# Two column chunks of a two-level Strassen-Winograd matmul made into one chunk of 2048 columns

## The chip, the cores and the metric

The kernel runs on one core of a Trainium2 chip, the other cores being idle. The metric is the device time of one execution in microseconds, lower is better. The kernel before was timed in three runs; the profile is of one execution.

## The reference

```python
def setup_inputs():
    m, k, n = 4096, 4096, 4096
    return {
        "a": np.random.randn(m, k).astype(np.float32),
        "b": np.random.randn(k, n).astype(np.float32),
        "bias": np.random.randn(n).astype(np.float32),
    }

def reference(a, b, bias):
    return np.tanh(np.matmul(a, b) + bias)
```

All of it is float32 in memory. The kernel converts a and b to fp16 as it loads them, and sums in float32.

## The kernel before, in words

**Chunks, pairs, duos.** The output has 4096 columns, in four chunks of 1024 (`NC`, `NCW`). Its 32 blocks of 128 rows make 16 pairs; two pairs make a duo, so there are 8 duos. For a pair and a chunk the product is one of 2 x 2 blocks: two blocks of rows, two halves of the 4096-long inner dimension, two halves of 512 columns.

**First level.** The Winograd form of Strassen's method needs seven block products in place of eight: P1 to P7. Each takes a left operand (a11, a12, a22 or one of the sums s1 = a21 + a22, s2 = s1 - a11, s3 = a11 - a21, s4 = a12 - s2) and a right operand (b11, b21, b22 or t1 = b12 - b11, t2 = b22 - t1, t3 = b22 - b12, t4 = b21 - t2). Done plainly, one product for one pair is 16 matmuls of 512 columns (`product`, line 786). The outputs are sums of the seven: P1 + P2 is one of the four blocks; P1 + P6 and then + P7 give intermediate values that feed the other three.

**Second level.** A duo has 2 pairs, so each of its first-level products is itself a product of 2 x 2 blocks (two pairs, two halves of the 2048-long inner dimension, two halves of 256 columns). `Fine` (line 1070) does it by the same seven-product form, p1 to p7, each 8 matmuls of 256 columns (`fine_product`, line 801; the matmul is line 808). Its left sums come from `fine_left` (line 633: with skewed storage a sum of 128x1024 and one of 128x2048), its right sums from `fine_right` (line 771: f1 to f4 of a right operand). A `Fine` step holds two banks of PSUM: `al` and `be`, in halves of 256 columns. `next_banks` (line 1142) deals four such twos in turn.

**Order of one step.** `step` (line 1276) overlaps neighbours: p1 of the new product, then p7 and p5 of the one before, then p2 and p6 of the new one, then p4 and p3 of the one before, and then the sums that read the finished banks of the one before.

**The four chunks.** The first chunk is done while a and b arrive, with first-level products; `STEEP` (line 59) says how many products of each duo use the second level. From the second chunk on nearly everything is second level. `pass_one` (line 1305) runs P1, P2 and P6 over all duos, `pass_two` (line 1388) runs P7, P5, P4, P3 duo after duo. Between the two passes each duo's running value, 512 KB, goes out to a DRAM scratch (`states`) and back. The duos' left operands lie in a DRAM scratch too; the second chunk forms s1, s3, s4 of those duos that lack them and stores them for later chunks (`HELD`, `keep`, `whole`, lines 1207 to 1212 and 1267 to 1271). For every chunk the left operands are fetched again by SP's DMA queue.

**What sets the order.** Nothing is issued as it is written: every operation is put on a list (`add`, line 156) with an assumed duration, its readers and writers, and a due time counted back from the end. `Plan.schedule` (line 226) plays this list forward, gives every tile one of 51 places of 4 KB per partition in SBUF (`PLACES`; an fp16 tile of 128x2048 is one place), and fixes the order on each engine and the order of DMA issues. `early` and `reach` say how far ahead of its due time an operation may take a place that others will need. Loads of b go through POOL's DMA queue (`load_b`, line 708, in four issues of 128 KB per block of 4 x 128 rows and 512 columns; the issue is line 720), at most eight under way (`RING`). Everything else goes through SP's queue. Sums of tiles and of banks are DVE's (`tt`, line 453, which the profile books at line 454), copies and tanh ACT's (line 457 and the activation lines).

**The end.** `step_last` (line 1293) takes the last product's quarters out one by one: a sum of 256 columns, tanh, and a store.

Of the kernel before, what the change touches and what calls it, by code (L numbers as in the profile page):

```python
# [10 lines left out]
P = 128  # L11
QP = 32
NB = 512
NH = NB // 2
NCW = 2 * NB
T = 16
TB = 4
# [14 lines left out]
NEAR = 11.0  # L32
REACH = 20.0
ORDER = ((2, 3, 4, 5, 6, 7), (7, 0, 4, 2, 6, 1, 3, 5), (2, 1, 4, 0, 3, 5, 6, 7), (7, 6, 5, 4, 3, 2, 1, 0))
SUMS = (0, 1, 2, 3, 4, 5, 6, 7, 8, 9, 10, 11, 12, 13, 14, 15)
SOFT = 1.5
BEHIND = 2
FARTHER = (50, 65, 40, 45)
# [17 lines left out]
SHARE = (0.31, 0.51, 0.43)  # L56
RISE = ((), (4, 4, 4, 4, 4, 4, 4, 4), (4, 4, 4, 4, 4, 4, 4, 4), (4, 4, 4, 4, 4, 4, 4, 4))
SECONDS = (0, 8, 8, 8)
STEEP = ((0, 1, 1, 1, 1, 2), (), ())
BASIS = ("a11", "a12", "a22", "s2")  # L60
STORED = BASIS + ("s1", "s3", "s4")
LEFT = ('P6', 'P7', 'P5', 'P4', 'P3')
Q_ORDER = (0, 2, 1, 3)


class Buf:
# [323 lines left out]
def kernel(  # L390
# [808 lines left out]
    def all_skewed(c, duo, pairs, fine):  # L1199
        a22 = Skew("a22", duo)  # L1200
        s2 = Skew("s2", duo, low="P6" not in fine and duo not in sixth)
        s3 = skew_sum("s3", a22, s2, SUB)
        a11 = Skew("a11", duo)
        s1 = skew_sum("s1", s2, a11, ADD, a11)
        a12 = Skew("a12", duo)
        s4 = skew_sum("s4", a12, s2, SUB, a12)
        have = {"a22": a22, "s2": s2, "s3": s3, "s1": s1, "s4": s4}
        for name in HELD:
            have[name].store(name, duo)
        for p in pairs:  # L1210
            held_names[p] = set(HELD)
            whole.add(p)
        return [have, have]

    def third(c, pq, pairs, fine):

        duo = min(pairs) // 2
        after = c + 1 < NC and RISE[c + 1][ORDER[c + 1][::-1].index(duo)] < 4
        if {"P7", "P4"} <= set(fine) and {("a22", duo), ("s2", duo)} <= skewed and not after:
            x = Skew("a22", duo)  # L1220
            y = Skew("s2", duo)
            for u, v in ((x.y, y.y), (x.x, y.x)):
                tt(at(v), at(u), at(v), SUB, T * P, (u, v), (v,), wide=False)
            for s in pq:
                s["a22"], s["s3"] = x, y
            if c < NC - 1:
                move("s3", duo, 0, y.y, 0, 2, True, soft=12.0)
                move("s3", duo, 2, y.x, 0, 2, True, soft=12.0)
                skewed.add(("s3", duo))
        else:  # L1230
            for s, p in zip(pq, pairs):
                s.update(fetch(("a22", "s2"), p))
                asum(s, "s3", "a22", "s2", SUB, over="s2")
                if c < NC - 1:
                    keep(p, s, ("s3",))
        for p in pairs:
            held_names[p].add("s3")

    def upper(pair):
# [9 lines left out]
    def others(c, pair, fine):  # L1249

        if pair in whole:
            return fetch(("s3", "s2", "s1", "a22", "s4"), pair)
        if pair in stored:
            s = fetch(("a22", "s2", "a11", "a12"), pair)
            asum(s, "s3", "a22", "s2", SUB)
            asum(s, "s1", "s2", "a11", ADD, over="a11")
        else:
            s = fetch(("a11", "a12"), pair)
            for name in ("a21", "a22"):
                natural_tile(pair, name, s, SOFT)  # L1260
# [6 lines left out]
        if c < NC - 1 and (pair in SUMS or c > 1):  # L1267
            spare = [name for p, name in (("P7", "s3"), ("P5", "s1"), ("P3", "s4")) if p in fine and name in KEPT[c]]
            keep(pair, s, HELD, spare=spare if pair % 2 else ())
            held_names[pair] = set(HELD)  # L1270
            whole.add(pair)
        return s

    waiting = []
# [113 lines left out]
    def pass_two(c, k, bop, rights, duos, on_chip):  # L1388


        def pre(tl):
            return lambda s: (at(tl, ALL, s), ((tl, (s,)),))

        for i, pairs in enumerate(duos):
            duo = min(pairs) // 2
            st = on_chip.get(duo)
            if not st:
# [62 lines left out]
            step(make("P7", pq, "s3", "t3"), after_seven)  # L1460
            if duo not in sixth:
                step(make("P6", pq, "s2", "t2", start=pre(st)), after_six)
            step(make("P5", pq, "s1", "t1", ramp(k, 1), lambda s: (at(k["b1"], ALL, s), ((k["b1"], (s,)),))), after_five)
            step(make("P4", pq, "a22", "t4", start=pre(st)), after_four)
            one = make("P3", pq, "s4", "b22", start=lambda s, cs=cs, in_cs=in_cs: (at(cs, ALL, s), (in_cs(s),)))
            if ends and "P3" in fine:
                step_last(one, last_quarter)
            else:
                step(one, after_three)

    early = set(range(4, NP)) | set(FIRST)

# [322 lines left out]
```

## Time and profile before

| | |
|---|---|
| three runs, us | 1447.21, 1445.84, 1445.7; median 1445.84 |
| span of the profiled execution, first to last instruction, us | 1444.5 |
| TensorE matmuls | 11424: 1434.9 us busy, 99% |
| VectorE (DVE) | 1784 instructions, 1143.4 us, 79% |
| ScalarE (ACT) | 1062 instructions, 453.5 us, 31% |
| GpSimd (POOL), DMA issues | 549 instructions, 295.5 us, 20% |
| DMA | 396.22 MB, mean 274 GB/s |
| granted TensorE clock, mean | 1.000 |

The profile has no time of its own beside the span: what lies around a span (launch, the last store's landing) is taken here as the runs' median less the span, 1445.84 - 1444.5 = 1.34 us. Reading it: a matmul's row in the timeline covers its whole way through the array, so rows of neighbours overlap, and the cost of one in a dense stream is the distance from start to start. `ps` is a bank of PSUM; x and y, v and z ahead of a name are the tiles and sums of a skewed left operand; f1 to f4 are second-level right sums. "Idle before, releaser" names what ended the idle time ahead of an instruction.

### The profile page before, as it was taken

The page shows a single profiled execution, that of the slowest core. Times are in us where ns is not written, and L with a number is a line of the kernel's source. Part 1 is how long each engine was busy: PE and PEld are TensorE (multiplying, and loading weights), DVE is VectorE, ACT ScalarE, POOL GpSimd, SP SyncE. Part 2 cuts the span into 40 slices and gives each one's busy share as a digit, 9 for nine tenths or more (in the row PEclk, how much of TensorE's full clock was granted, in tenths as well). Part 3 has the DMA queues.
Part 4 walks back from the last instruction along what each step waited for, and adds up shares of the span by engine and source line. Part 5 has one row for each costly group of instructions (what it writes and reads, how often), then busy time and mean ns, then how long its engine had stood idle before and what let it go on. Part 6 is the DMA issues. An engine that isn't in the chain of part 4 may idle for free.

```text
span 1444.5 us, 29352 instructions
## 1 busy us (share of the span) xinstructions
PE 1434.9 (99%) x11424; PEld 1116.2 (77%) x11424; DVE 1143.4 (79%) x1784; ACT 453.5 (31%) x1062; POOL 295.5 (20%) x549
## 2 busy tenths in 40 slices
PE   9999999999999999999999999999999999999998
PEld 4444545554578888888888888888888888888887
DVE  3449968777966889998898799976779589986765
ACT  3111211211233322434333332343343332243433
POOL 8754333334424002000120300000220310000000
PEclk9999999999999999999999999999999999999999
DMA  9999999999999897999999998778999988687872
GB/s 177 196 230 259 299 307 304 301 275 271 254 278 254 271 297 179 331 406 366 327 332 375 293 288 279 242 247 288 252 302 330 261 238 290 224 276 244 273 253 103
DMA packets 198315, 396.22 MB, mean 274 GB/s; under 512 B 25888, under 2 KB 89888, under 8 KB 198176
## 3 DMA queue, kind: packets, MB, share of 16 engines
q1 hardware_dynamic: 117792, 323.01, 63.8%
q0 software_dynamic: 80384, 71.34, 31.3%
q8 instruction: 89, 1.46, 0.4%
q14 instruction: 50, 0.41, 0.1%
HBM read 324.53 MB, written 141.03 MB: 322 GB/s over the span
## 4 chain that ended last, share of the span: by engine, by line
PE 76%; DMA 10%; DVE 4%; issue 1%; POOL 1%; ACT 0%; SPq 0%; DVEq 0%; POOLq 0%
PE ps L808 66%; PE ps L793 10%; DMA b<-in_b_dram 4%; DMA nat<-in_a_dram 2%; DMA out_dram<-parts 1%; DMA s<-a 1%; DMA out_dram<-p 1%; DMA s<-s 1%; DMA xa<-a 1%; DVE parts L454 0%; DMA a<-ya 0%; DVE s L454 0%; DVE a L486 0%; POOL nat L510 0%; DVE a L454 0%
## 5 line engine op out<-in xcount | busy, mean ns | idle before, releaser
L720 POOL DMA_DIRECT2D b<-in_b_dram x256 | 137.5, 541 | 589.2 <-DMA out_dram<-st 192.6
L457 ACT COPY ps<-ps 128x256 f32<-128x256 f32 (+1 forms) x304 | 111.3, 366 | 393.6 <-PE ps L808 379.6
L510 POOL DMA_DIRECT2D nat<-in_a_dram x224 | 120.8, 543 | 274.9 <-PE ps L808 125.6
L808 PEld LDWEIGHTS <-zs 128*128 128x128 f16 x1536 | 150.1, 98 | 17.8
L808 PEld LDWEIGHTS <-ys 128*128 128x128 f16 x1440 | 140.8, 98 | 16.4
L808 PEld LDWEIGHTS <-ya 128*128 128x128 f16 x1328 | 129.8, 98 | 15.2
L808 PEld LDWEIGHTS <-xs 128*128 128x128 f16 x1248 | 122.0, 98 | 14.6 <-issue 0.3
L808 PEld LDWEIGHTS <-za 128*128 128x128 f16 x1232 | 120.4, 98 | 15.5 <-issue 1.4
L457 ACT COPY parts<-ps 128x256 f32<-128x256 f32 (+1 forms) x192 | 74.2, 388 | 163.7 <-DVE ps L454 63.4
L808 PEld LDWEIGHTS <-parts 128*128 128x128 f16 x1152 | 112.6, 98 | 13.2
L793 PEld LDWEIGHTS <-s 128*128 128x128 f16 x608 | 59.4, 98 | 72.6 <-issue 2.7
L454 DVE TENSOR_TENSOR parts<-ps,parts 128x256 f32<-128x256 f32 (+1 forms) x180 | 79.0, 439 | 43.2 <-PE ps L808 34.6
L808 PEld LDWEIGHTS <-xa 128*128 128x128 f16 x1056 | 103.2, 98 | 12.7 <-issue 0.6
L1575 PE MATMUL ps<-b,o 128*128 128x512 f16 x512 | 111.3, 379 | 0.1
L646 DVE TENSOR_TENSOR zs<-xs,ys 128x2048 f16<-128x2048 f16 x78 | 95.2, 1220 | 18.5 <-PE ps L808 10.9
L793 PEld LDWEIGHTS <-a 128*128 128x128 f16 x576 | 56.2, 98 | 67.0 <-DVE a L454 1.0
L454 DVE TENSOR_TENSOR ps<-ps,parts 128x256 f32<-128x256 f32 (+1 forms) x196 | 86.9, 445 | 25.3 <-PE ps L808 18.7
L808 PE MATMUL ps<-b,zs 128*128 128x256 f16 x784 | 101.6, 273 | 0.0
L1575 PEld LDWEIGHTS <-o 128*128 128x128 f16 x512 | 49.7, 98 | 60.5 <-issue 0.6
L486 DVE STREAM_TRANSPOSE a<-nat 128x512 uint32<-128x512 uint32 x112 | 72.8, 687 | 29.8 <-PE ps L793 14.1
L808 PE MATMUL ps<-f1t,parts 128*128 128x256 f16 x672 | 87.1, 273 | 0.0
L793 PE MATMUL ps<-t,s 128*128 128x512 f16 x384 | 84.3, 379 | 2.2 <-DVE ps L454 2.2
(132 smaller groups left out, 2564.7 us busy)
## 6 DMA issues: line engine op xcount, KB each, us to landing
ys<-s SPq DMA_DIRECT2D x78, 512.0 KB, 5.0
xs<-s SPq DMA_DIRECT2D x78, 512.0 KB, 5.4
ya<-a SPq DMA_DIRECT2D x66, 512.0 KB, 6.9
xa<-a SPq DMA_DIRECT2D x66, 512.0 KB, 7.5
b<-in_b_dram POOLq DMA_DIRECT2D x256, 128.0 KB, 7.8
out_dram<-parts SPq DMA_DIRECT2D x112, 256.0 KB, 6.6
nat<-in_a_dram POOLq DMA_DIRECT2D x224, 128.0 KB, 9.2
a<-a SPq DMA_DIRECT2D x32, 512.0 KB, 8.1
```

Of the source, the lines that this page charges most:

```text
L454: dve(n, lambda: nc.vector.tensor_tensor(out=o(), in0=x(), in1=y(), op=op), reads, writes, wide, **kw)
L457: act(n, lambda: nc.scalar.copy(o(), x()), reads, writes, **kw)
L486: nc.vector.transpose(dst[ALL].rearrange("P t m -> P (t m)").bitcast(pair32).rearrange("P (U m) -> P U m", m=P)[:, ds(t0 // 2, nu), ds(row ...
L510: nc.gpsimd.dma_start(out=tl[(ds(q * QP, QP), *key)], in_=src)
L646: nc.vector.tensor_tensor(out=halves(z), in0=halves(x), in1=halves(y)[:, ds(0, 1)].broadcast_to([P, 2, TP * P]), op=SUB,)
L720: nc.gpsimd.dma_start(out=dst.rearrange("p t j n -> p t (j n)") if j is None else dst, in_=src)
L793: nc.tensor.matmul(bank[ALL], left_tile(left, k + t + shift), rb.tile(t), start=start and k == t0 and t == 0, stop=k + t == t0 + nt - 1, s ...
L808: nc.tensor.matmul(bank[ALL, HALF[half]], left_tile(buf, at_ * TP + i * TB + t), rb.tile(t), start=False, stop=i == 1 and t == TB - 1, ski ...
L1575: nc.tensor.matmul(bank[ALL], left_tile(left, t), rb.tile(tb), start=start, stop=stop, skip_group_check=True,)
```

## The change

The first two chunks keep their form. The third and fourth become one chunk of 2048 columns, done by a new function `wide_pass`. A first-level half is then 1024 columns, a second-level quarter 512: each second-level product is 8 matmuls of 512 columns into a whole bank, and a step holds four banks. The order is no longer duo after duo: each product runs over all duos before the next starts (a turn), forward and backward in alternation; P6 with P7, and P5 with P3, share a turn in which the second follows one duo behind. The intermediate values U1 (P1), U2 (U1 + P6), U3 (U2 + P7) and V go from turn to turn, in SBUF where the next use is at most four steps off (`TURN`), otherwise through DRAM. Right operands are made once per turn from b, which is loaded for b11, b21, b22 and b12, and again for b21 (P4) and b22 (P5, P3). The second chunk stores no s1, s3, s4 any more (`LASTING`); where a duo lacks them the wide pass forms them again. `STEEP` of the first chunk's last duo goes from 2 to 3: its P5 is second-level too. In the second chunk the last three duos of `pass_two` run product by product together (`TOGETHER`).

```diff
-SUMS = (0, 1, 2, 3, 4, 5, 6, 7, 8, 9, 10, 11, 12, 13, 14, 15)
+LASTING = ((), (), (), ())
+SHARED = True
...
-STEEP = ((0, 1, 1, 1, 1, 2), (), ())
+STEEP = ((0, 1, 1, 1, 1, 3), (), ())
...
+WIDE = 2
+TOGETHER = (0, 3, 0, 0)
+WIDE_ORDER = (0, 1, 2, 3, 4, 5, 6, 7)
+WIDE_PASSES = ((("P1", 0),), (("P2", 0),), (("P6", 0), ("P7", 1)), (("P4", 0),), (("P5", 0), ("P3", 1)))
+TURN = 4
+WIDE_EARLY = {"P1": (11.0, 60), "P2": (11.0, 60), "P6": (11.0, 100), "P7": (11.0, 100), "P4": (11.0, 60), "P5": (11.0, 60), "P3": (11.0, 60)}
...
+        todo = list(enumerate(duos))
+        cut = len(todo) - TOGETHER[c]
+        for lot in [[x] for x in todo[:cut]] + [todo[cut:]]:
+            runs = [products(*x) for x in lot]
+            while runs:
+                runs = [r for r in runs if next(r, r) is not r]
...
+    class Wide:
...
+            self.u, self.a, self.b, self.d = sets.pop(0)
+            sets.append((self.a, self.d, self.u, self.b))
...
+                        nc.tensor.matmul(
+                            bank[ALL, cols], left_tile(buf, at_ * TP + i * TB + t), rb.tile(t, half),
+                            start=start and not (i or t), stop=i == 1 and t == TB - 1, skip_group_check=True,
+                        )
...
+        def first(self):
+            if self.const:
+                pre, _, deps = self.const
+                copy(at(self.u), pre, NB, deps, (self.u,))
+            self.run(self.u, "p1", not self.const)
+            copy(at(self.a), at(self.u), NB, (self.u,), (self.a,))
+
+        def second(self):
+            self.v = new("u", [P, NB], fp32, "out")
+            self.run(self.a, "p2")
+            self.run(self.u, "p6")
...
+                copy(at(self.b), at(self.u), NB, (self.u,), (self.b,))
+            copy(at(self.v), at(self.u), NB, (self.u,), (self.v,))
+
+        def third(self):
+            v = self.v
+            self.run(self.u, "p7")
+            tt(at(v), at(self.u), at(v), SUB, NB, (self.u, v), (v,))
+            self.run(self.b, "p5")
+            tt(at(self.d), at(self.b), at(v), ADD, NB, (self.b, v), (self.d,))
+
+        def fourth(self, between):
+            self.run(self.u, "p4")
+            between()
+            self.run(self.b, "p3")
...
+    NEEDS = {"P1": (), "P2": ("U1",), "P6": ("U1",), "P7": ("U2",), "P4": ("U3",), "P5": ("U2", "U3"), "P3": ("V",)}
+    MAKES = {"P1": "U1", "P6": "U2", "P7": "U3", "P5": "V"}
+    LEFTS = {"P1": "a11", "P2": "a12", "P6": "s2", "P7": "s3", "P4": "a22", "P5": "s1", "P3": "s4"}
...
+        def split(name, kept):
+            fine = {}
+            for i in range(2):
+                q11, q12, q21, q22 = (raw[name, r + i, h] for r in (0, 2) for h in (0, 1))
+                f1, f2, f4 = (block(f"{f}{name}") for f in ("f1", "f2", "f4"))
+                f3 = block(f"f3{name}") if kept else q12
+                for o, x, y in ((f1, q12, q11), (f2, q22, f1), (f3, q22, q12), (f4, q21, f2)):
+                    combine(o, x, y, SUB, soon[0])
...
+            if p in ("P6", "P7"):
+                if ("t3", 0, 0) not in raw:
+                    for part in parts:
+                        for name in ("b22", "b12"):
+                            load(name, [part])
+                        total("t3", "b22", "b12", SUB, "b12", [part])
+                        total("t2", "t3", "b11", ADD, "b11", [part])
+                return split("t2", True) if p == "P6" else split("t3", False)
+            if p == "P4":
+                for part in parts:
+                    load("b21", [part])
+                    total("t4", "b21", "t2", SUB, "b21", [part])
+                return split("t4", False)
+            if p == "P5":
+                for part in parts:
+                    load("b22", [part])
+                    total("t1", "b22", "t2", SUB, "t2", [part])
+                return split("t1", False)
+            return split("b22", False)
...
+        def sum_into(o, src, s, h, bank, half=None):
...
+            tt(
+                at(o[s], *key), mine, at(src[s], *key), ADD, NB if half is None else NH,
+                (bank, (src[s], span(h, half))), ((o[s], span(h, half)),), soft=3.0,
+            )
...
@@ -1687,6 +2063,11 @@
+        if c >= WIDE:
+            if c == WIDE:
+                wide_pass(c)
+                before = held = None
+            continue
```

Left out are the functions that fetch or form the left operands (`wide_left`), store and reload the intermediate values (`keep_value`, `value`), set tanh and the store of a row (`out_row`, `out_part`), and the last step (`wide_last`, which takes the last subproduct in two halves of 256 columns).

More of the change, by code (lines that the diff above doesn't have):

```diff
@@ L1207, in all_skewed @@
         have = {"a22": a22, "s2": s2, "s3": s3, "s1": s1, "s4": s4}
-        for name in HELD:
+        for name in LASTING[c]:
             have[name].store(name, duo)
         for p in pairs:
-            held_names[p] = set(HELD)
-            whole.add(p)
+            held_names[p] = set(LASTING[c])
         return [have, have]
@@ L1225, in third @@
                 s["a22"], s["s3"] = x, y
-            if c < NC - 1:
+            if "s3" in LASTING[c]:
                 move("s3", duo, 0, y.y, 0, 2, True, soft=12.0)
@@ L1233, in third @@
                 asum(s, "s3", "a22", "s2", SUB, over="s2")
-                if c < NC - 1:
+                if "s3" in LASTING[c]:
                     keep(p, s, ("s3",))
-        for p in pairs:
+        for p in pairs if "s3" in LASTING[c] else ():
             held_names[p].add("s3")
@@ L1266, in others @@
         asum(s, "s4", "a12", "s2", SUB, over="a12")
-        if c < NC - 1 and (pair in SUMS or c > 1):
+        if LASTING[c]:
             spare = [name for p, name in (("P7", "s3"), ("P5", "s1"), ("P3", "s4")) if p in fine and name in KEPT[c]]
-            keep(pair, s, HELD, spare=spare if pair % 2 else ())
-            held_names[pair] = set(HELD)
-            whole.add(pair)
+            keep(pair, s, LASTING[c], spare=spare if pair % 2 else ())
+            held_names[pair] = set(LASTING[c])
         return s
@@ L1392, in pre, with products @@
             return lambda s: (at(tl, ALL, s), ((tl, (s,)),))
-        for i, pairs in enumerate(duos):
+        def products(i, pairs):
             duo = min(pairs) // 2
@@ L1460, in pass_two @@
             step(make("P7", pq, "s3", "t3"), after_seven)
+            yield
             if duo not in sixth:
                 step(make("P6", pq, "s2", "t2", start=pre(st)), after_six)
+                yield
             step(make("P5", pq, "s1", "t1", ramp(k, 1), lambda s: (at(k["b1"], ALL, s), ((k["b1"], (s,)),))), after_five)
+            yield
             step(make("P4", pq, "a22", "t4", start=pre(st)), after_four)
+            yield
             one = make("P3", pq, "s4", "b22", start=lambda s, cs=cs, in_cs=in_cs: (at(cs, ALL, s), (in_cs(s),)))
@@ L1469, in pass_two, with combine @@
                 step(one, after_three)
+        todo = list(enumerate(duos))
[4 more added lines that the diff above has]
+                runs = [r for r in runs if next(r, r) is not r]
+    def combine(o, x, y, op, early=0.0):
+        (ob, ok, oa), (xb, xk, xa), (yb, yk, ya) = (v.part(0, 1) for v in (o, x, y))
+        tt(
+            at(ob, *ok), at(xb, *xk), at(yb, *yk), op, TB * NB,
+            ((xb, xa), (yb, ya)), ((ob, oa),), wide=False, early=early,
+        )
@@ new lines, with __init__, run, emit @@
+    sets = []
+    class Wide:
+        def __init__(self, pq, name, right, duo, const=None):
+            self.left, self.right = fine_left(pq, name, duo, False), right
+            if not sets:
+                for i in (0, 2):
+                    x, y = (banks[2 * n:2 * n + 2] for n in ring[i:i + 2])
+                    sets.append((x[0], x[1], y[0], y[1]))
+            self.u, self.a, self.b, self.d = sets.pop(0)
+            sets.append((self.a, self.d, self.u, self.b))
+            self.const = const
+            self.here = ((0, 0, self.a), (1, 1, self.d), (1, 0, self.u), (0, 1, self.b))
+        def run(self, bank, p, start=False, half=None):
+            buf, at_ = self.left[p]
+            cols = ALL if half is None else HALF[half]
+            for i in range(2):
+                rb = self.right[p, i]
+                def emit(i=i, rb=rb):
+                    for t in range(TB):
+                        nc.tensor.matmul(
+                            bank[ALL, cols], left_tile(buf, at_ * TP + i * TB + t), rb.tile(t, half),
+                            start=start and not (i or t), stop=i == 1 and t == TB - 1, skip_group_check=True,
+                        )
+                add("PE", TB * (0.2158 if half is None else 0.1092), emit, ((buf, (at_,)) if len(buf.atoms) > 1 else buf, *rb.deps()), (bank,))
+        def first(self):
[8 more added lines that the diff above has]
+            self.run(self.u, "p6")
+            if self.const:
+                _, edge_, deps = self.const
+                tt(at(self.b), at(self.u), edge_, ADD, NB, (self.u, *deps), (self.b,))
+            else:
+                copy(at(self.b), at(self.u), NB, (self.u,), (self.b,))
[10 more added lines that the diff above has]
+            self.run(self.b, "p3")
@@ new lines, in wide_step, with rest, wide_last @@
+    def wide_step(one, after):
+        one.first()
+        if waiting:
+            waiting.pop()(one.second)
+        else:
+            one.second()
+        def rest(between, later=lambda: None):
+            one.third()
+            between()
+            one.fourth(later)
+            for s, h, bank in one.here:
+                after(s, h, bank)
+        waiting.append(rest)
+    def wide_last(one, after):
+        one.first()
+        waiting.pop()(one.second, one.third)
+        after(0, 0, one.a)
+        after(1, 1, one.d)
+        one.run(one.u, "p4")
+        after(1, 0, one.u)
+        for half in range(2):
+            one.run(one.b, "p3", half=half)
+            after(0, 1, one.b, half)
@@ new lines, with wide_sequence @@
+    NEEDS = {"P1": (), "P2": ("U1",), "P6": ("U1",), "P7": ("U2",), "P4": ("U3",), "P5": ("U2", "U3"), "P3": ("V",)}
+    MAKES = {"P1": "U1", "P6": "U2", "P7": "U3", "P5": "V"}
+    LEFTS = {"P1": "a11", "P2": "a12", "P6": "s2", "P7": "s3", "P4": "a22", "P5": "s1", "P3": "s4"}
+    def wide_sequence(order):
+        seq, turns, flip = [], [], False
+        for n, p in enumerate(WIDE_PASSES):
+            line = order[::-1] if flip else order
+            flip = not flip
+            for i in range(len(line) + max(lag for _, lag in p)):
+                seq += [(name, line[i - lag]) for name, lag in p if 0 <= i - lag < len(line)]
+            turns += [n] * (len(seq) - len(turns))
+        return seq, turns
@@ new lines, with wide_left @@
+    shared = {}
+    def wide_left(name, pairs):
+        pq, duo = [{}, {}], min(pairs) // 2
+        if name in BASIS or name in held_names.get(pairs[0], ()):
+            fetch_fine(pq, name, pairs, True)
+            if name == "s2" and SHARED:
+                shared[duo] = pq
+            return pq
+        x, y, op, over = {"s3": ("a22", "s2", SUB, 1), "s1": ("s2", "a11", ADD, 1), "s4": ("a12", "s2", SUB, 0)}[name]
+        if {(x, duo), (y, duo)} <= skewed:
+            u, v = (shared[duo][0]["s2"] if n == "s2" and duo in shared else Skew(n, duo) for n in (x, y))
+            if name == "s1" and SHARED:
+                shared[duo] = [{"s2": u}, {"s2": u}]
+            else:
+                shared.pop(duo, None)
+            s = skew_sum(name, u, v, op, (u, v)[over])
+            return [{name: s}, {name: s}]
+        mine = shared.get(duo, pq)
+        for s, p, m in zip(pq, pairs, mine):
+            s.update(fetch([n for n in (x, y) if n not in m], p))
+            s.update({n: m[n] for n in (x, y) if n in m})
+            asum(s, name, x, y, op, over=(x, y)[over])
+        if name == "s1" and SHARED:
+            shared[duo] = [{"s2": s["s2"]} for s in pq]
+        else:
+            shared.pop(duo, None)
+        return pq
```

160 lines of the change are left out of this document (added).

## The prediction

> **What bounds the kernel now.** I read the page first, then the list of what TensorE waited for, then its timeline, then the other engines and the DMA queues in the stretch that is rewritten. The page and the waits:
>
> ```profile
> span 1444.5 us, 29352 instructions
> PE 1434.9 (99%) x11424; PEld 1116.2 (77%) x11424; DVE 1143.4 (79%) x1784; ACT 453.5 (31%) x1062; POOL 295.5 (20%) x549
> ```
>
> ```profile
> PE ps L793 <- DVE ps L454: 2.2, 2, 2.0
> PE warm L1495 <- DVE zeros L1489: 1.4, 1, 1.4
> PE ps L808 <- ACT parts L457: 0.9, 1, 0.9
> PE ps L793 <- DVE a L454: 0.5, 1, 0.5
> PE ps L808 <- DVE ps L454: 0.2, 1, 0.2
> ```
>
> TensorE (PE) is busy for 1434.9 of 1444.5 us, and all its waits together are 5.2 us (2.2 + 1.4 + 0.9 + 0.5 + 0.2). So PE is the bound in every stage, and the time moves only if PE has less to stream or begins to wait. Is a busy PE also dense? Its timeline gives the spacing of both kinds of matmul, start to start. First-level products, 512 columns:
>
> ```profile
> 280.86 13.98 PE L793 MATMUL ps<-t,s 128*128 128x512 f16 x64
> 294.68 7.07 PE L793 MATMUL ps<-b,a 128*128 128x512 f16 x32
> 301.58 3.62 PE L793 MATMUL ps<-b,s 128*128 128x512 f16 x16
> 305.04 7.07 PE L793 MATMUL ps<-t,a 128*128 128x512 f16 x32
> 311.94 1.04 PE L808 MATMUL ps<-b,a 128*128 128x256 f16 x8
> ```
>
> Second-level products, 256 columns, in octets; 40 octets lie from the first row to the second:
>
> ```profile
> 1399.85 1.04 PE L808 MATMUL ps<-t,ya 128*128 128x256 f16 x8
> ...
> 1434.78 1.04 PE L808 MATMUL ps<-f4t,xa 128*128 128x256 f16 x8
> ```
>
> 144 wide matmuls take 311.94 - 280.86 = 31.08 us, 215.83 ns each. 320 narrow ones take 1434.78 - 1399.85 = 34.93 us, 109.16 ns each. Two narrow ones cost 218.32 ns, so one wide matmul does the same columns 2.49 ns cheaper. The third and fourth chunk (line 808 alone, then all engines):
>
> ```profile
> 755.00:1440.00 685.00, 684.89 (x6274) 1.00 0.84 267
> ```
>
> ```profile
> 755.00:1440.00 685.00, 684.89 (x6274) 612.94 (x6273) 547.62 (x871) 250.89 (x611) 52.98 (x99) 1.00 0.84 267
> ```
>
> The columns are length, busy time by engine (PE, weight loads, DVE, ACT, POOL), granted clock, DMA share, GB/s. Two chunks of 8 duos x 7 products x 7 subproducts x 8 matmuls are 6272; they fill these 685 us without a hole, at clock 1.00, with DVE at 80% and DMA at 0.84.
>
> **The change part by part.** *Matmuls.* The wide pass does the same 49 subproducts per duo once, on 512 columns: 8 x 49 x 8 = 3136 matmuls, of which the last eight are cut in halves (16 of 256 columns). 3128 x 215.83 + 16 x 109.16 = 676.9 us in place of 6272 x 109.16 = 684.7 us: **-7.8 us**. All of it is on the path, since PE is the path.
>
> *STEEP 2 to 3.* The last duo of the first chunk does P5 by 56 narrow matmuls (6.11 us) in place of 32 wide ones (6.91 us): **-0.8 us**. It adds right-hand sums for t1 (8 subtractions of 128x1024) and left-hand ones to DVE near 350 to 410 us, three more places just as the second chunk's b arrives; bounds: all 0.8 us lost again, or all kept. I keep it.
>
> *PSUM.* A step now holds four banks and two sets alternate, where four sets of two did. In a step of 12.1 us (7 x 8 x 215.83 ns) PE runs p1 of this duo, p7 and p5 of the one before, p2 and p6, then p4 and p3 of the one before. The tightest cover is p1, then an ACT copy, then p2: 3.45 us of the other duo's matmuls (16 x 215.83 ns) lie between, 1.75 us (16 x 109.16) before. The copies and sums:
>
> ```profile
> L457 ACT COPY ps<-ps 128x256 f32<-128x256 f32 x192 | 68.7, 358 | 251.6 <-PE ps L808 250.5
> L457 ACT COPY st<-ps 128x512 f32<-128x512 f32 x32 | 18.6, 582 | 4.2 <-PE ps L808 3.7 <-DMA xa<-a 0.5
> ```
>
> ```profile
> L646 DVE TENSOR_TENSOR zs<-xs,ys 128x2048 f16<-128x2048 f16 x60 | 73.2, 1221 | 17.5 <-PE ps L808 10.2 <-DMA out_dram<-st 4.0 <-DMA out_dram<-cs 1.6
> L454 DVE TENSOR_TENSOR st<-ps,st 128x512 f32<-128x512 f32 x65 | 43.8, 686 | 3.9 <-PE ps L808 3.9
> L454 DVE TENSOR_TENSOR parts<-ys 128x1024 f16<-128x1024 f16 x60 | 41.0, 684 | 0.4 <-PE ps L808 0.3
> L454 DVE TENSOR_TENSOR t<-b,t 128x2048 f16<-128x2048 f16 x16 | 19.5, 1220 | 2.6 <-PE ps L808 2.6
> ```
>
> The copy grows from 358 to about 582 ns while its cover doubles: nothing. A bank's last use lies 10 us ahead of its next (p4 of step n to the copy in step n + 2), against 0.69 + 0.58 us of work. If DVE falls behind by those 9 us, PE stops; so DVE's load matters.
>
> *DVE.* Left sums 56 x (0.684 + 1.221) = 107 us; s3, s1, s4 formed again for the five duos that no longer store them, 5 x 3 x 2 x 1.22 = 37; right blocks 7 x 8 x 1.22 = 68; t1 to t4 32 x 1.22 = 39; banks 44 x 8 x 0.686 = 242. Sum 493 of 677 us, 73% against 80% now: off the path, if no single subtraction blocks its queue. ACT has fewer, wider copies, and stays near a third.
>
> *DMA.* By the program, left operands are fetched once (5 duos x 8 + 3 x 7 sets of 1 MiB = 61 MiB, in place of 2 x 8 x 7 = 112), b in six quarters of 8 blocks (b21 and b22 twice), 192 loads in place of 128. U1, U2, U3 go out (6 + 8 + 6 MiB) and come back (12 + 8 + 12), 52 MiB in place of 14; outputs stay 32 MiB. Now, in 755 to 1440 us:
>
> ```profile
> q1 hardware_dynamic: 57417, 168.20, 71.3%
> q0 software_dynamic: 15078, 13.72, 12.6%
> ```
>
> That is 2.90 us of all 16 engines per MB on q1 and 6.29 on q0. After: 145 MiB or 152 MB x 2.90 + 192 x 0.131 MB x 6.29 = 599 us of 677, share 0.88. The second chunk's stretch ran at 0.97 with PE busy for 347.73 of 349 us:
>
> ```profile
> 406.00:755.00 349.00, 347.73 (x3128) 305.57 (x3127) 308.24 (x476) 123.06 (x301) 50.30 (x94) 1.00 0.97 304
> ```
>
> So the mean rate costs nothing. SP issues fewer, larger transfers. The s1, s3, s4 stores that LASTING takes out of this stretch free DMA where PE waits about 1 us in all: at most a few tenths. TOGETHER only reorders the last three duos of the second chunk; its price is read at the start of the wide pass, between 0 (the starts of the third and fourth chunk, in the 685 us above) and 1.05 us (0.85 + 0.20, the start of the second chunk, below). I take 0.
>
> *Turns.* What is new is five turns (P1, P2, P6 with P7, P4, P5 with P3), each with right-hand blocks twice as large, in the same 51 places of SBUF. b comes through POOL's queue. Its issues where they are dense (12 from the first row to the last), the landing of one where they queue, and what such a queue has cost PE so far:
>
> ```profile
> 740.42 0.55 POOL L720 DMA_DIRECT2D b<-in_b_dram  x1 [1.80 <-DMA b<-in_b_dram]
> ...
> 757.48 0.54 POOL L720 DMA_DIRECT2D b<-in_b_dram  x1 [0.82 <-DMA b<-in_b_dram]
> ```
>
> ```profile
> 385.55 11.82 DMA b<-in_b_dram
> ```
>
> ```profile
> 414.22 1.03 PE L808 MATMUL ps<-f3b,za 128*128 128x256 f16 x8 [0.85 <-ACT parts L457]
> ...
> 451.41 1.03 PE L808 MATMUL ps<-f3b,za 128*128 128x256 f16 x8 [0.20 <-DVE ps L454]
> ```
>
> An issue takes 17.06 / 11 = 1.55 us, a block of four 6.2 us, a landing 11.8 us. I counted places, a tile's life over the step time, from the program. In the P6/P7 turn right blocks hold 16 + 14, bias and edge 2, left operands about 7.4, U tiles about 7.5: 47 of 51. b21 for P4 needs 8. Let T be the start of the last P6 step. Its first f blocks come free at T + 8.6 us (end of p6), P4 wants its own f2 at T + 36.3 + 6.9 = T + 43.2. If n of the 8 blocks were loaded before, f2 is ready at T + 8.6 + (8 - n) x 6.2 + 11.8 + 5 x 1.22 (one t4 and four f sums), so PE waits **32.9 - 6.2 n** us: 8.1 at n = 4, 1.9 at n = 5, nothing from 6. Behind the waiting p6 stands all of PE; behind the waiting subtraction stands DVE's queue, with the sums that empty the last P7 banks. The ends are 0 and 32.9 us. The count says 4 free places; a fifth comes as the reloads of U1 run out. I take n = 5: **+1.9 us**. The other turns: P1 leaves about 8 places free for P2's successors, P4 about 5; nothing, as at the starts of the third and fourth chunk.
>
> *Tail.* The last halves go through the same chain of 256-column sum, tanh and store as now:
>
> ```profile
> 1440.52 0.42 DVE L454 TENSOR_TENSOR cs<-ps,cs 128x256 f32<-128x256 f32 x1 [0.45 <-PE ps L808]
> 1440.56 1.19 SPq L1446 DMA_DIRECT2D out_dram<-cs  x2
> 1440.97 0.42 ACT L1443 ACTIVATE cs<-cs 128x256 f32<-128x256 f32 x1 [0.46 <-DVE cs L454]
> ```
>
> Sum: -7.8 - 0.8 + 1.9 = -6.7 us; span 1437.8. The runs' median is 1.3 us above the profiled span (1445.84 against 1444.5), which stays: **1439.1 us**.
>
> **The rivals.** A measurement here tells about 0.2% (2.9 us) from no change, so faster ends at 1442.9 and slower begins at 1448.7.
>
> *Same.* n = 4, or 6 to 11 us of small waits over the five turns: 1445.84 - 8.6 + 8.1 = 1445.3. For: 47 of 51 is a mean, and means are exceeded. Against: the turns of now cost 1.05 us at worst.
>
> *Slower: b21 comes late at the turn to P4.* If three or fewer blocks fit ahead, PE waits 14.3 us (n = 3) to 32.9 (n = 0): 1451.5 to 1470; it decides from 11.5 us, n below 3.5. For: this turn holds the most right blocks and the U tiles of two products. Against: right and left tiles die in pieces, and the schedule is laid with places in view. The trace never shows PE idle longer than the 2.0 us above, and the clock at 1.00 throughout. The Trainium skill, "TensorE: Matmul & The Clock Gate", Part 1, says the matmul clock falls to half after an idle window of about 3.4 us and needs about as long a busy one to come back: by it each wait of this length costs about 1.7 us more (an estimate), and at n = 3 the time would be 1453. No run so far has an idle stretch that long, so it is not shown here.
>
> *Slower: b12 and b22 late at the turn to P6.* 64 loads are 64 x 1.55 = 99 us against a P2 turn of 96.7 us (8 x 12.1). If none starts in P1, f2 is ready 99 + 11.8 + 6 x 1.22 = 118 us into the turn and wanted at 103.6: 14.5 us, 1451.7. It decides unless half a block or more is early; P1's free places speak against.
>
> *It does not do what it says.* A 512-column matmul of the second level costs twice a narrow one: only STEEP is left, 1445.84 - 0.8 + 1.9 = 1446.9. Against: line 793 already shows the spacing.
>
> **How the numbers follow.** Forecast (waits up to 5.7 us) 0.58, its own range 1437.2 to 1442.9; same 0.16; late b21 0.20; late b12 and b22 0.04; no saving 0.02. Faster 0.58, same 0.18, slower 0.24. Below, little is left: with no wait it is 1437.2, and about 1 us for a tail or early waits that shrink gives 1436. Above, the range takes in n = 3 with a little more, to 1454, and leaves out about 0.13.
>
> **What would show it.** The spacing of the wide pass near 215.8 ns, x3128 of 128x512; DVE near 490 us in it; PE's waits in five places, at the turns, the longest before f2 of t4 (right block of P4) and ended by DVE behind a b21 landing. The forecast is wrong if PE waits more than 6 us in sum, if waits stand inside a turn (banks or DVE), or if the first two chunks change by more than 1 us.

## The result and the profile after

The changed kernel takes 1442.26 us (median of 20 runs, 1440.81 to 1449.56) against 1447.37 us (20 runs, 1444.36 to 1451.06): ratio 0.997, 95% interval 0.9962 to 0.9979, that is 4.3 us less, between 3.0 and 5.5. Forecast were 6.7 us less. The kernel before came out a little slower than in its first three runs, so the ratio and not the two medians is compared. The profiled execution of the changed kernel has a span of 1440.0 us against 1444.5.

The page after, first span and engines, then the list of what TensorE (PE) waited for:

```profile
span 1440.0 us, 22221 instructions
PE 1426.3 (99%) x8320; PEld 813.8 (57%) x8320; DVE 1076.0 (75%) x1534; ACT 385.6 (27%) x727; POOL 330.2 (23%) x613
```

```profile
PE ps L815 <- DVE ps L461: 5.3, 5, 2.5
PE warm L1871 <- DVE zeros L1865: 1.4, 1, 1.4
PE ps L800 <- DVE a L461: 1.1, 1, 1.1
PE ps L1519 <- DVE u L461: 0.5, 1, 0.5
PE ps L1951 <- DMA b<-in_b_dram: 0.4, 1, 0.4
PE ps L815 <- ACT ps L464: 0.4, 1, 0.4
PE ps L815 <- ACT parts L464: 0.4, 1, 0.4
PE ps L1951 <- DVE o L1996: 0.3, 1, 0.3
```

The new line numbers: 815 is the narrow second-level matmul, 800 the first-level one, 1519 the wide pass. PE lost its narrow matmuls (11424 instructions became 8320) and 8.6 us of work, and its waits grew from 5.2 to 9.8 us. Line 1519, which is new and half of the run, has 0.5 us of them. Where the others lie shows PE's timeline (start, length, and in brackets the idle time and its releaser):

```profile
228.56 3.63 PE L800 MATMUL ps<-b,a 128*128 128x512 f16 x16 [1.09 <-DVE a L461]
...
409.06 1.03 PE L815 MATMUL ps<-b,a 128*128 128x256 f16 x8 [0.39 <-ACT ps L464]
414.34 1.03 PE L815 MATMUL ps<-f3b,za 128*128 128x256 f16 x8 [2.50 <-DVE ps L461]
452.51 1.03 PE L815 MATMUL ps<-f3b,za 128*128 128x256 f16 x8 [1.34 <-DVE ps L461]
530.06 1.03 PE L815 MATMUL ps<-f4t,xs 128*128 128x256 f16 x8 [0.48 <-DVE ps L461]
742.49 1.03 PE L815 MATMUL ps<-b,zs 128*128 128x256 f16 x8 [0.39 <-ACT parts L464]
746.97 1.03 PE L815 MATMUL ps<-f4b,xs 128*128 128x256 f16 x8 [0.82 <-DVE ps L461]
753.44 1.03 PE L815 MATMUL ps<-f4b,a 128*128 128x256 f16 x8 [0.20 <-DVE ps L461]
...
1435.35 1.03 PE L1519 MATMUL ps<-b,zs 128*128 128x256 f16 x8 [0.51 <-DVE u L461]
```

Most of it is at the start of the second chunk (409 to 453 us), at the end of the second chunk (742 to 753) and on the last eight matmuls; 1.1 us lies in the first chunk and 0.5 in the middle of the second. Between 755.18 us, the wide pass's first matmul, and 1435 us PE does not stop once, though it takes four turns of right-hand blocks in that stretch. Its spacing, over 42 octets:

```profile
1085.01 1.89 PE L1519 MATMUL ps<-f2t,ys 128*128 128x512 f16 x8
...
1157.53 1.89 PE L1519 MATMUL ps<-f2t,ya 128*128 128x512 f16 x8
```

(1157.53 - 1085.01) / 336 = 215.83 ns, to the digit what line 793 had shown. The other engines and the DMA share in the wide pass and in the second chunk (columns as in the prediction):

```profile
755.00:1436.00 681.00, 680.49 (x3178) 310.71 (x3176) 472.50 (x610) 179.07 (x269) 86.18 (x160) 1.00 0.85 260
406.00:755.00 349.00, 342.69 (x3084) 301.45 (x3083) 313.64 (x483) 124.38 (x301) 51.74 (x96) 1.00 0.91 269
```

DVE has 472.5 us in the wide pass, 69% (493 us and 73% were forecast), DMA 0.85 (0.88 forecast).

So where did the gain go? The wide pass, 755.18 to 1436.2 us, less the four narrow octets of the old chunk in it (3.5) and the 0.5 of wait, is 677.0 us of matmuls in place of 684.7: -7.7. P5 at the second level, as worked out: -0.8. Against that stand waits: +2.2 up to 460 us (7.5 against 5.3), +0.5 to 690 us, +1.4 at the end of the second chunk, +0.5 on the last matmuls; the time behind the last matmul shrank by 0.4. Sum -4.3; measured -4.5.

### The profile page after: what moved, and what is told of

Same layout as the page of the kernel before. It is cut to its first block, busy times and chain, and to the rows that moved or that the text cites. A ratio compares the mean times of both kernels' runs of the same rounds, so it can differ in the third digit from the quotient of the medians.

```text
span 1440.0 us, 22221 instructions
## 1 busy us (share of the span) xinstructions
PE 1426.3 (99%) x8320; PEld 813.8 (57%) x8320; DVE 1076.0 (75%) x1534; ACT 385.6 (27%) x727; POOL 330.2 (23%) x613
## 3 DMA queue, kind: packets, MB, share of 16 engines
q8 instruction: 65, 1.06, 0.3%
## 4 chain that ended last, share of the span: by engine, by line
PE 76%; DMA 14%; DVE 5%; POOL 2%; issue 2%; ACT 0%; DVEq 0%; SPq 0%; POOLq 0%; ACTq 0%
PE ps L1519 47%; PE ps L815 17%; PE ps L800 8%; DMA nat<-in_a_dram 5%; DMA b<-in_b_dram 5%; PE ps L1951 4%; DMA a<-a 1%; DMA xa<-a 1%; POOL land L517 1%; POOL b L727 1%; DMA out_dram<-parts 1%; DVE ps L461 1%; DVE a L461 0%; DVE parts L461 0%; DVE ys L461 0%
## 5 line engine op out<-in xcount | busy, mean ns | idle before, releaser
L464 ACT COPY ps<-ps 128x512 f32<-128x512 f32 (+1 forms) x209 | 97.7, 468 | 448.0 <-PE ps L1519 303.3
L461 DVE TENSOR_TENSOR u<-ps,u 128x512 f32<-128x512 f32 (+1 forms) x161 | 106.4, 683 | 45.5 <-PE ps L1519 44.2
L461 DVE TENSOR_TENSOR parts<-ps,parts 128x512 f32<-128x512 f32 (+1 forms) x125 | 70.8, 567 | 85.2 <-PE ps L1519 72.1
L461 DVE TENSOR_TENSOR ps<-ps,parts 128x512 f32<-128x512 f32 (+1 forms) x144 | 80.0, 558 | 38.5 <-PE ps L1519 31.5
L1519 PE MATMUL ps<-b,zs 128*128 128x512 f16 (+1 forms) x456 | 106.0, 375 | 0.5 <-DVE u L461 0.5
L1519 PEld LDWEIGHTS <-zs 128*128 128x128 f16 x520 | 50.9, 98 | 60.5 <-issue 0.7
L800 PE MATMUL ps<-b,a 128*128 128x512 f16 x352 | 78.1, 379 | 1.1 <-DVE a L461 1.1
L1519 PEld LDWEIGHTS <-ya 128*128 128x128 f16 x480 | 47.0, 98 | 56.6
L1519 PE MATMUL ps<-b,za 128*128 128x512 f16 x320 | 75.6, 379 | 0.0
L461 DVE TENSOR_TENSOR b<-b,b 128x2048 f16<-128x2048 f16 (+2 forms) x66 | 66.8, 1024 | 11.6 <-DMA b<-in_b_dram 11.4
L1519 PEld LDWEIGHTS <-ys 128*128 128x128 f16 x416 | 40.7, 98 | 49.1
```

What stands on the lines that cost most here:

```text
L461: dve(n, lambda: nc.vector.tensor_tensor(out=o(), in0=x(), in1=y(), op=op), reads, writes, wide, **kw)
L464: act(n, lambda: nc.scalar.copy(o(), x()), reads, writes, **kw)
L800: nc.tensor.matmul(bank[ALL], left_tile(left, k + t + shift), rb.tile(t), start=start and k == t0 and t == 0, stop=k + t == t0 + nt - 1, s ...
L1519: nc.tensor.matmul(bank[ALL, cols], left_tile(buf, at_ * TP + i * TB + t), rb.tile(t, half), start=start and not (i or t), stop=i == 1 and ...
```

## The experiments

My theory after that: the wide pass gives what its matmuls save and no more, and it needs TOGETHER to start without a hole; P5's step to the second level pays its 0.8 us back in waits. The rivals: the gain comes from fewer sums and copies, TOGETHER is only a reordering, and the longer waits come from a new order of everything (the planner counts due times back from the end). Idle time of PE below is a stretch's length less PE's busy time in it.

**The changed kernel again**, as the measure.

> The changed kernel unaltered, as the measure for the others of this batch. Span near 1440.0 us, 4 to 5 us under the kernel before; waits of TensorE near 9.9 us in all, about 4.2 us of them between 405 and 455 us.

Ratio 0.9961 (0.9948 to 0.9974), span 1439.2 us; 3.3 us idle from 400 to 460 us, 1.35 from 690 to 760, none from 760 to 1430.

**P5's step, undone and alone.**

```diff
-STEEP = ((0, 1, 1, 1, 1, 3), (), ())
+STEEP = ((0, 1, 1, 1, 1, 2), (), ())
```

> Undoes one part: the last duo of the first chunk does P5 by first-level matmuls again. Theory (P5's extra DVE work and places cause the longer waits at the start of the second chunk): matmuls +0.8 us, waits between 405 and 455 us back from 4.2 to about 1.05 us, so 2.4 us under the changed kernel, span near 1437.6. Rival (the waits come from the new order of everything, as due times are counted back from another end): waits stay near 4.2 us, span near 1440.8.

> One part alone: the kernel before with P5 of the first chunk's last duo at the second level. Theory: matmuls -0.8 us, waits between 405 and 455 us up by 3.2 us from 1.05, so 2.4 us over the kernel before, span near 1446.9. Rival (the order of everything): -0.8 us, span near 1443.7.

> The changed kernel with P5 of the first chunk's last duo at the first level, a second time. If P5's second level brings nothing, as it did not in the kernel before: ratio to the kernel before 0.9955 to 0.9965, 0 to 1.5 us under the changed kernel. If it costs what one profile showed: 2.4 us under it.

Undone: 0.9956 (0.994 to 0.9972) and, the second time, 0.996 (0.9946 to 0.9975), where the changed kernel had 0.997 and 0.9961. Alone in the kernel before: 1.0001 (0.9993 to 1.001), span 1445.9. So the step is worth nothing that shows. Standing alone it did not cost 2.4 us (that would be a ratio of 1.0017); a gain of 0.8 us (0.9994) lies just inside the interval and is not excluded. Undone, the waits between 405 and 455 us were 2.3 and 1.5 us, between the theory's 1.05 and the rival's 4.2. The longest group of its waits in the kernel before:

```profile
PE ps L808 <- DVE ps L454: 4.4, 7, 1.1
...
```

Of the 4.4 us only 1.0 lies between 400 and 460 us, the rest later. That spoke against my theory as it stood. The rival can be settled from the traces: the instructions of all kernels with the same STEEP stand in the same order on every engine until 594 us, whether they have the wide pass or not. So the new order is no cause, and one profile is not enough to read a difference of 2 us there. All profiles together, idle from 0 to 460 us: seven with STEEP at 2 (the kernel before among them) have 3.65 to 5.3 us, mean 4.7; seven with 3 have 3.7 to 7.5, mean 5.7. By these means P5's second level costs about 1.0 us of waits and saves 0.8, but the two groups overlap widely, so that 1.0 is not shown beyond the spread. In the profile after, 7.5 is the longest of its seven: with a mean cost of 1.0, the other 1.2 of the +2.2 us up to 460 is what single executions happened to draw.

**Narrow matmuls in the wide pass.** Everything else as in the changed kernel.

```diff
-                        nc.tensor.matmul(
-                            bank[ALL, cols], left_tile(buf, at_ * TP + i * TB + t), rb.tile(t, half),
...
+                        for h in (range(2) if half is None else (half,)):
+                            nc.tensor.matmul(
+                                bank[ALL, HALF[h]], left_tile(buf, at_ * TP + i * TB + t), rb.tile(t, h),
...
```

> The changed kernel with each 512-column matmul of the wide pass cut into two of 256 columns; order, tiles, banks and transfers as they are. Theory (the gain of the wide pass is the cost per matmul): 3128 x 2.49 ns = 7.8 us longer, span near 1447.5, no new waits in the wide pass. Rival (the gain comes from fewer sums, copies and transfers): under 2 us longer.

1447.88 us against 1447.29 of the kernel before: 1.0006 (0.9994 to 1.0019). The whole gain is gone. Its wide pass, first start and last:

```profile
752.36 1.91 PE L1520 MATMUL ps<-b,a 128*128 128x256 f16 x16
...
1440.35 1.03 PE L1520 MATMUL ps<-b,zs 128*128 128x256 f16 x8 [0.52 <-DVE u L461]
```

From 752.36 to 1440.35 are 687.99 us; in the changed kernel from 755.18 to 1435.35 are 680.17. The difference is 7.8 us, as worked out, and there is no new wait. The rival (fewer sums, copies, transfers) falls: with narrow matmuls the new arrangement is worth nothing. Each narrow matmul also loads its weights anew, so what is shown is the cost of a matmul together with its weight load; no run separates the two.

**Without TOGETHER, and with two and four duos**, the latter two with STEEP at 2.

```diff
-TOGETHER = (0, 3, 0, 0)
+TOGETHER = (0, 0, 0, 0)
...
+TOGETHER = (0, 2, 0, 0)
...
+TOGETHER = (0, 4, 0, 0)
```

> Undoes one part: the last three duos of the second chunk run one after the other again. Theory (the product-by-product order lets right blocks die early and makes room for b11 of the wide pass): without it the 16 blocks of P1 find no room until the last duo, b11 is late, and TensorE waits 5 to 30 us between 740 and 790 us. Rival (only a reordering): within 1 us of the changed kernel, and the 1.4 us of waits that it has between 740 and 755 us may go.

> STEEP at 2 as in steep2, and two duos in place of three run product by product at the end of the second chunk. Theory (room for b11 of the wide pass grows with the number of duos that finish a right operand together): waits between 690 and 800 us lie between those with three duos (1.1 to 2.7 us) and with none (9.8 us, and some 3 us of half clock): 3 to 8 us, span 1440 to 1445. Rival (any number from two on does it): under 2.7 us.

> STEEP at 2, and four duos together. Theory: right blocks die no later than with three, waits between 690 and 800 us at most 2.7 us, span 1437 to 1440. Rival (four duos' running values and left operands take the room): waits over 4 us there.

None: 1.0041 (1.0027 to 1.0056), slower than the kernel before. Two: 1.0037 (1.0023 to 1.0051). Four: 0.995 (0.9932 to 0.9969), as with three. PE's waits without TOGETHER, then its timeline there:

```profile
PE ps L1519 <- DMA b<-in_b_dram: 5.7, 1, 5.7
PE ps L1519 <- DVE f2b L461: 4.1, 1, 4.1
```

```profile
762.70 1.86 PE L1519 MATMUL ps<-b,a 128*128 128x512 f16 x4 [5.72 <-DMA b<-in_b_dram]
764.36 1.91 PE L1519 MATMUL ps<-f2b,ya 128*128 128x512 f16 x4
770.35 1.87 PE L1519 MATMUL ps<-f2b,ya 128*128 128x512 f16 x4 [4.08 <-DVE f2b L461]
772.01 1.89 PE L815 MATMUL ps<-f4b,xa 128*128 128x256 f16 x8
773.72 1.06 PE L815 MATMUL ps<-b,zs 128*128 128x256 f16 x8
```

P1 waits first for b11 itself and then for its f2. POOL's issues of b11 say why; there are 32 of them, four to each of eight blocks. The row with the first and the row with the thirteenth, without TOGETHER and then in the changed kernel:

```profile
679.55 2.14 POOL L727 DMA_DIRECT2D b<-in_b_dram  x4 [101.68 <-PE ps L815]
...
733.69 4.33 POOL L727 DMA_DIRECT2D b<-in_b_dram  x8 [42.85 <-PE ps L815]
```

```profile
702.99 2.68 POOL L727 DMA_DIRECT2D b<-in_b_dram  x5 [123.64 <-PE ps L815]
...
715.22 3.74 POOL L727 DMA_DIRECT2D b<-in_b_dram  x7 [2.39 <-PE ps L815]
```

Without TOGETHER three of the eight blocks go out even earlier, but the other five wait 42.85 us for a matmul, whose end frees a place. The thirteenth issue comes 18.5 us later than in the changed kernel, and the last at 756.22 us in place of 741.88. That fits the theory, that right blocks die sooner when three duos run P7, P5, P4, P3 together; the trace names the matmul that was waited for, not the blocks. The rival's second half was right too: without TOGETHER PE does not wait once from 690 to 755.9 us, so the 1.4 us at 742 to 753 us come with TOGETHER.

With two duos the thirteenth issue goes out at 724.39 us and the last at 750.99, with four at 711.28 and 742.38. From three on PE's waits from 690 to 800 us are 1.1 to 2.7 us. With two they are no shorter than with none (13.4 and 9.8 us): 4.0 of them lie before the wide pass, and 9.4 at its start, the longest (7.0) for an f2 that DVE began only at 770.88, after it had stood until 761.07 us and then worked through its queue without a pause. That the wait falls step by step was wrong; why DVE comes so late with two stays open.

**b11 earlier**, STEEP at 2.

```diff
-WIDE_EARLY = {"P1": (11.0, 60),
+WIDE_EARLY = {"P1": (11.0, 100),
```

> STEEP at 2, and the loads of b11 for P1 may start 100 us ahead in place of 60. If the waits at the start of the wide pass come from late issues of these loads: under 0.5 us between 690 and 800 us, span near 1437. If they come from places or from DVE's queue: as in steep2, 1.1 to 2.7 us.

0.9957 (0.9939 to 0.9976); 1.6 us idle from 690 to 760 us, where the changed kernel with STEEP at 2 had 1.1 and 2.7, and 1.8 us new between 800 and 1100. The last b11 issue went out at 726.29 us in place of 739.48, so the waits left ahead of the wide pass are not from late permission to load.

**b21 late.**

```diff
-"P4": (11.0, 60)
+"P4": (11.0, 1)
```

> The loads of b21 for P4 may start at most 1 us ahead of their due time instead of 60. By the formula of the prediction, with F the first b21 issue counted from the start T of the last P6 step, TensorE waits F + 49.6 + 11.8 + 6.1 - 43.2 = F + 24.3 us ahead of f2: for F between -10 and +8.6 that is 14 to 33 us, span 1454 to 1473, and where a wait is longer than about 3.4 us the granted clock falls in the windows behind it, for 1 to 2 us more each. Rival (b's queue is faster than 1.55 us an issue when nothing else is needed, or the first subproducts run on the first blocks): half of that or less.

1.0096 (1.0072 to 1.012), span 1460.5. The last P6 step starts at T = 1104.3 us; the first b21 issue came at 1124.06, F = 19.8, later than I had thought, and by the formula PE should wait 44 us. It waited 1.1, 6.4, 6.8 and 0.3:

```profile
PE ps L1519 <- DVE b L461: 7.8, 2, 6.7
PE ps L1519 <- DMA b<-in_b_dram: 6.4, 1, 6.4
...
```

The rival's "half or less" it was. The f2 that p6 needs was ready at T + 60.7, 26.6 us ahead of the formula's T + 87.3: 16.2 of that are the issues, 6.9 the last landing (4.9 us in place of 11.8), 3.5 the sums. The 32 issues went out from 1124.06 to about 1158 us, 1.06 us each; the first 16 were 1.10 us apart while PE still ran without a pause, so 1.55 was too long even there. While PE stood the queue went faster still:

```profile
1152.37 5.67 POOL L727 DMA_DIRECT2D b<-in_b_dram  x9 [1.15 <-DMA b<-in_b_dram]
```

Nine issues in 5.67 us, 0.63 us each, 208 GB/s. In the window in the middle of it (its last three figures are clock, DMA share and GB/s) no queue but b's moved anything, and its packets fill the 16 DMA engines (packets, MB, share of the 16 engines):

```profile
1155.00:1160.00 5.00, 0.40 (x1) 0.50 1.23 198
```

```profile
q0 software_dynamic: 1086, 0.99, 123.2%
```

So the formula's 1.55 us an issue and 11.8 us a landing are those of two crowded stretches of the kernel before, and the wait came out a third of what they gave: while PE stands, the other queue falls silent here, and a wait for b shortens itself.

**s1, s3, s4 stored again**, with STEEP at 3 and at 2.

```diff
-LASTING = ((), (), (), ())
+LASTING = ((), ("s1", "s3", "s4"), (), ())
```

> Undoes one part: the second chunk stores s1, s3 and s4 of five duos again and the wide pass fetches them. Theory (that transfer is off the path): DVE in the wide pass 37 us less, DMA share between 460 and 755 us back up by 0.05 to 0.1, time within 1.5 us of the changed kernel. Rival (the transfers freed there keep the start of the wide pass free of longer waits): waits between 690 and 760 us up from 1.4 by 2 us or more.

> STEEP at 2, and s1, s3, s4 stored by the second chunk and fetched by the wide pass. Two parts that brought nothing, both undone: ratio to the kernel before 0.995 to 0.997, as the changed kernel; no new waits in the wide pass.

0.996 (0.9945 to 0.9975) and 0.9941 (0.9923 to 0.9959): as the changed kernel. The same stretches as above, with the stores:

```profile
755.00:1436.00 681.00, 677.58 (x3154) 308.35 (x3152) 436.34 (x569) 177.41 (x267) 86.40 (x160) 1.00 0.84 257
406.00:755.00 349.00, 345.02 (x3105) 303.53 (x3103) 313.85 (x485) 125.80 (x305) 51.82 (x96) 1.00 0.98 302
```

DVE in the wide pass falls by 36 us (37 were expected), the DMA share of the second chunk rises from 0.91 to 0.98, and no wait grows by 2 us. Both are off the path. The kernel with both parts undone has the lowest ratio of all, 0.9941. Its interval lies just below that of the changed kernel's first measurement (0.9962 to 0.9979) and overlaps that of the second (0.9948 to 0.9974); whether it is better than the change stays open.

## Why the prediction was right, and where not

The direction and the cause were right, and the time lies in the forecast's own range. That it came so near owes something to luck: of its three terms only the first came about as worked out, and the 1.9 us of b21 that did not come made up for part of 4.6 us of other waits, which the sum had at nothing. One of the prediction's own signs of being wrong did appear: the first two chunks changed by more than 1 us (4.1 us more waits: 2.2, 0.5 and 1.4). Its picture of the waits, at the turns and the longest before f2 of t4, was wrong as well: PE did not wait at any turn inside the wide pass.

- **Matmuls, -7.8 us: right**, and the only source of the gain. Spacing 215.83 ns, 677.0 against 676.9 us, and 7.8 us lost again with narrow matmuls.
- **STEEP, -0.8 us, "I keep it": not borne out.** The other end of the bound is nearer: seven profiles against seven have about 1.0 us more of waits, and alone it measured 1.0001 (0.9993 to 1.001).
- **b21, +1.9 us: the count right, the size not.** In the changed kernel T is 1102.3 us. 20 of the 32 issues (five blocks) had gone out by T + 8.6, so n = 5:

```profile
992.24 2.27 POOL L727 DMA_DIRECT2D b<-in_b_dram  x4 [81.87 <-PE ps L1519]
1066.48 4.29 POOL L727 DMA_DIRECT2D b<-in_b_dram  x8 [71.97 <-PE ps L1519]
...
1102.74 2.14 POOL L727 DMA_DIRECT2D b<-in_b_dram  x4 [25.18 <-DVE ys L461]
1115.41 2.14 POOL L727 DMA_DIRECT2D b<-in_b_dram  x4 [10.53 <-DVE ys L461]
1120.01 2.14 POOL L727 DMA_DIRECT2D b<-in_b_dram  x4 [2.46 <-PE ps L1519]
...
1128.30 0.54 POOL L727 DMA_DIRECT2D b<-in_b_dram  x1 [0.49 <-DMA b<-in_b_dram]
```

The last issue was at T + 26.0 (27.2 by the formula), and the sums behind its landing, on DVE:

```profile
1140.19 1.22 DVE L461 TENSOR_TENSOR b<-b,b 128x2048 f16<-128x2048 f16 x1
1141.51 1.23 DVE L461 TENSOR_TENSOR f2t<-b,f1t 128x2048 f16<-128x2048 f16 x1
```

  The landing took 9.9 us, and the t4 stood 2.0 us more behind other sums in DVE's queue, together about the 11.8 of the formula, by chance. But only two sums (one t4, one f2) were left, not five: the other blocks' sums had been made while it was under way. f2 was there at T + 40.5, 2.7 us ahead of p6. The step that failed is "5 x 1.22".
- **TOGETHER, 0 to 1.05 us, "I take 0": the weakest step.** The wait at its place is 1.35 to 1.4 us in the two profiles of the changed kernel, beyond the upper end, and without it the change would have been slower than the kernel before. I had looked for the turn that decides in P4, where the rival "slower" stood; its mechanism (right blocks that find no place, a late b) is real, but at the turn into the wide pass.
- **The tail, no change: nearly.** The two last halves of 256 columns now share one bank with each other, and the second has to let the first one's sum pass: 0.5 us. Before, the last subproduct was one group of 256 columns.
- **Banks, DVE, DMA at nothing: right**, 680 us without a wait inside the wide pass.
- **The 1.3 us around the span:** in the profiled execution after they are 1.7 (1441.7 against 1440.0), which the forecast of the median has 0.4 too low.
- The forecast's -6.7 us was 2.2 us more than the profile's -4.5: +2.2 for the waits up to 460 us (1.0 of it P5's by the means of seven), +0.5 to 690, +1.4 just ahead of the wide pass, +0.1 for the tail (0.5 of wait, 0.4 less behind it), -1.9 for b21: together 2.3.

## What to carry to other kernels

TensorE was dense here, and the fixed cost of a matmul with its weight load was all that the wider tile saved: 2.5 ns for each two that become one. Count it before writing a new pass, and take the number as the ceiling. Then look at the one hand-over into the new pass, not only at the turns inside it: large operands need places that the old stage must have freed, and the order of the old stage's last rows decided here between 0.3% faster and 0.4% slower. Waits of 1 to 3 us differ that much between executions of the same instructions (up to 460 us 3.7 to 7.5 us in seven profiles); judge them from several profiles.

## What the runs showed of the hardware

**The clock falls during a wait of some microseconds.** Without TOGETHER, TensorE's granted clock in stretches of 5 us (length, PE busy, clock, DMA share, GB/s):

```profile
755.00:760.00 5.00, 1.98 (x15) 1.00 1.12 322
760.00:765.00 5.00, 2.30 (x6) 0.51 1.12 310
765.00:770.00 5.00, 1.27 (x3) 0.81 0.52 149
770.00:775.00 5.00, 4.65 (x22) 0.66 0.05 10
775.00:780.00 5.00, 5.00 (x24) 1.00 0.92 283
```

After 5.7 us of idling the clock is 0.51: four 512-column matmuls take 764.36 - 762.70 = 1.66 us, 415 ns each in place of 216, and eight of 256 columns behind the second wait take 773.72 - 772.01 = 1.71 us in place of 0.87. Up to the clock's return the matmuls behind the two waits lose 1.8 and 1.7 us. With the 8.4 us of added waits (9.8 less 1.4) and 0.9 us fewer waits before 690 us that makes 11.0; the span grew by 10.8. For these two waits this bears out the Trainium skill, "TensorE: Matmul & The Clock Gate", Part 1, which has the clock halve after an idle window of about 3.4 us and return after about as long a busy one; the prediction's estimate from it, 1.7 us a wait, is what this run gave. But 3.4 us of waiting was not needed every time. After the 2.50 us wait at 414 us of the changed kernel the octets keep their 0.87 us; in the run with b21 late, a wait of 2.34 us at the same place is followed by a lower clock:

```profile
415.06 1.34 PE L815 MATMUL ps<-f3b,za 128*128 128x256 f16 x8 [2.34 <-DVE ps L461]
...
419.34 1.04 PE L815 MATMUL ps<-f2b,ya 128*128 128x256 f16 x8
```

```profile
415.00:420.00 5.00, 4.95 (x31) 0.66 1.17 270
```

Three octets take 419.34 - 415.06 = 4.28 us in place of 2.62: here too 1.7 us are lost. What decides between two such waits, no run here shows.

**A load queue is as fast as its neighbours let it be.** The same issues of b came 1.55 us apart in the kernel before at 740 to 757 us, where SP's transfers took 63% of the 16 DMA engines' time, 1.10 us apart in the run with b21 late at 1124 to 1140 us, where they took 42.5%, and 0.63 us when nothing else moved.
